# Reciprocal roots spread over the partitions by transposes of a column read with step zero, in place of a diagonal and an fp32 product

## The chip, the cores and the metric

The kernel runs on one core of a Trainium2 chip. The metric is the device time of one execution in microseconds (us); lower is better. Three runs of the kernel before gave 3015.92, 3015.95 and 3016.99 us, a median of 3015.95.

The engines of the core that matter here are PE (TensorE, the matrix engine, whose loads of the stationary operand are listed apart as PEld), DVE (VectorE), ACT (ScalarE), POOL (GpSimd) and SP (SyncE, which issues the transfers).

## The reference

One step of a two-layer hybrid encoder for 1024 prompt tokens and 64 sample tokens, in fp32. Layer 0 is a Mamba-2 state-space mixer (SSD) and a SwiGLU FFN, layer 1 a chunk-band attention and a second FFN. Every sub-layer stands between two RMS norms, and the SSD's output is normalised once more within each of four groups of channels:

```python
def rmsnorm(x, w):
    y = x * lax.rsqrt(jnp.mean(x * x, axis=-1, keepdims=True) + EPS)
    return y * w

# ssd_mixer, after the scan
yg = y.reshape(b, L, SSM_GROUPS, D_INNER // SSM_GROUPS)
yg = yg * lax.rsqrt(jnp.mean(yg * yg, axis=-1, keepdims=True) + EPS)
return (yg.reshape(b, L, D_INNER) * gnorm_w) @ w_out

# each layer
x = x + rmsnorm(mixer(rmsnorm(x, nw[0])), nw[1])
x = x + rmsnorm(swiglu(rmsnorm(x, nw[2]), ffn_w_in, ffn_w_out), nw[3])
```

The model width is 1024, the inner width of the SSD 2048.

## The kernel before

**Layout.** Features lie on the 128 partitions and tokens along the free axis, 1088 of them. Projections take them in three slices of 384, 384 and 320 tokens (`SL`), the out projections in four quarters of 256, 256, 288 and 288 (`QS`). Both operands of a matmul are split in a high and a low part, so that each tile takes three matmuls of type fp32r (lines 455 to 457, 1271 to 1273 and 1470 to 1472). The FFN uses products of sums of blocks, seven in place of eight.

**A norm's factor.** The sum of squares over features is a sum over partitions. `rstd` (L483) makes it with matmuls against a column of ones, 128 tokens at a time, into a PSUM tile `nst`. So the sums lie with tokens on partitions, one column for each 128 tokens, and nine small DVE operations (the last one L504) turn them into reciprocal roots, all but a constant factor `RL`. The column is a tile `nr`, or, for the group norms of the SSD, a place in `rst`. What follows needs the root of each token along the free axis and the same on all partitions. Before the change that takes three steps:

- `diag` (L506, its operation L508): DVE multiplies the identity with the column, block by block, which gives up to three diagonal matrices of 128x128 side by side in a tile `dg` of a ring of two (`DG`).
- `bcast` (L513, its product L516): PE multiplies a constant matrix, filled with `RL` (`frac`), with the diagonals, in fp32. All rows of the product are the roots.
- ACT copies the product from its PSUM tile `nbp` into `rb` (L520), which DVE multiplies with the data. `rb` has one buffer unless the caller gives one.

`nst` and `nbp` come out of one ring of two PSUM tiles (`ax`).

There are 44 such broadcasts: 28 from `rb_steps` (L523), which runs `rstd`, `diag` and `bcast` with pauses between for the norms in front of and behind the sub-layers (`start_norm` for the first norm, `chain` between a mixer and its FFN, `end` behind an FFN), and 16 from `build_y` (L584), for the group norms.

**Order.** PE's order is written out by hand. The main loops issue the matmuls of the projections and add their cost to a virtual clock, `st` (a `Stream`, L89). Side tasks are generators: a task yields its own cost, a delay and, where it needs one, a condition, and goes on when the virtual clock has passed the delay and the condition holds. So a delay sets how many matmuls of the main loop stand on PE between two steps of a task. The delays of `rb_steps` ahead of its broadcast are given for each caller by tables (`wait`, or else `RB_WAIT`). The other engines are ordered by priorities; `HIP` is a high one.

**`build_y`** prepares the SSD's output for its out projection: eight times (a quarter with half of the features) two blocks of four feature tiles. For a block it waits until two tiles of the ring `R` are free and the statistics of its tokens are there, broadcasts the block's roots, loads four raw tiles through SP's queue, multiplies them on DVE (L601), and writes a high part on ACT (L602) and a low part on DVE (L603), the operands of the out projection (`project`, L608). The statistics come from the SSD's tasks, which add the squares into `ssg` (L928) and call `rstd`.

**The last norm.** In `end`, for the last slice of layer 1 (`more` given), PE's matmuls `hold` (L1364) put the residual into PSUM tiles `xp` between the steps of `rb_steps`, and the scaled result is added to it there (L1373, L1375).

Of the kernel before, what the change touches and what calls it, by code (L numbers as in the profile page):

```python
# [8 lines left out]
F32 = mybir.dt.float32  # L9
F32R = mybir.dt.float32r  # L10
I32 = mybir.dt.int32
AF = mybir.ActivationFunctionType
ALU = mybir.AluOpType
# [3 lines left out]
P = 128  # L17
# [23 lines left out]
RB_WAIT = 4.8  # L41
# [9 lines left out]
HIP = 3000  # L51
# [3 lines left out]
RWP = 3000, 0, 0  # L55

KBUF = 5
DGB = 2
RAWB, HLB, SGB = 2, 3, 5
NR, NRX = 16, 13  # L60

# [6 lines left out]
RL, RP = 0.274060676, (-5.145514965, 10.804858208, -11.997578621, 8.987062454)  # L68
# [305 lines left out]
def hybrid_kernel(  # L374
# [5 lines left out]
    V, A, G, PE = nc.vector, nc.scalar, nc.gpsimd, nc.tensor  # L380
# [3 lines left out]
    def pool(es, name, bufs=1, **kw):  # L384
        return es.enter_context(tc.tile_pool(reuse_waits="tile", name=name, bufs=bufs, **kw))

    cp = pool(ctx, "cp")
# [3 lines left out]
    nsb = pool(ctx, "nsb")  # L391
# [3 lines left out]
    ident = cp.tile([P, P], F32, name="ident")  # L395
    make_identity(nc, ident)
    ones = cp.tile([P, P], F32, name="ones")
    G.memset(ones, 1.0)
    frac = cp.tile([P, P], F32, name="frac")
    G.memset(frac, RL)  # L400
    pcs = cp.tile([P, NPC], F32, name="pcs")
    A.activation(ones[:, 0:1], ones[:, 0:1], AF.Square)

# [3 lines left out]
    rst = cp.tile([P, NCH, NG], F32, name="rst")  # L407
# [9 lines left out]
    R = Ring(rp, "r", NR, [P, 1152])  # L417
# [5 lines left out]
    W.tc, W.lent = tc, Lent(RX)  # L423
    W.raws.append(W.lent)
    UC = Cells(384, (R, 99))
    DG = Ring(nsb, "dg", DGB, [P, 3, P])

    def v4(t, n):
        return t[:, :4 * n].rearrange("p (k n) -> p k n", k=4)

    def rr(ap):
        return ap.bitcast(F32R)

    def col(c):
        return pcs[:, c:c + 1]

    def ax(name):
        return pax.tile([P, 512], F32, tag="ax", name=name)

    def mm(name):  # L440
        return pmm.tile([P, 512], F32, tag="mm", name=name)
# [61 lines left out]
            V.scalar_tensor_tensor(a, a, RP[2], h, op0=ALU.add, op1=ALU.mult)  # L503
            V.scalar_tensor_tensor(r, a, RP[3], y, op0=ALU.add, op1=ALU.mult)  # L504

    def diag(r3, nb):  # L506
        dg = DG.get()
        V.tensor_tensor(  # L508
            dg[:, :nb], ident.unsqueeze(1).to_broadcast([P, nb, P]), r3.unsqueeze(2).to_broadcast([P, nb, P]), op=ALU.mult
        )  # L510
        return dg

    def bcast(dg, a, n, rb=None):  # L513

        bp = ax("nbp")
        PE.matmul(bp[:, :n], frac, dg.rearrange("p a b -> p (a b)")[:, a:a + n], start=True, stop=True)  # L516
        DG.put()
        if rb is None:
            rb = nsb.tile([P, 384], F32, tag="rb", bufs=1, name="rb")
        A.copy(rb[:, :n], bp[:, :n])  # L520
        return rb[:, :n]

    def rb_steps(ssum, n, out, wait=None, rb=None, more=None):  # L523

        nb = (n + P - 1) // P
        nr = nsb.tile([P, 4], F32, tag="nr", bufs=2, name="nr")
        rstd(ssum, 1.0 / D, nr[:, :nb], nb, more)
        yield 0.2, 0, DG.free
        with tc.high_priority(HIP):
            dg = diag(nr[:, :nb], nb)  # L530
        yield 0.1, wait or RB_WAIT
        with tc.high_priority(HIP):
            out.append(bcast(dg, 0, n, rb))
        yield 0.5, 0

    def apply_split(src, rb, wcol, n, dh, dl, eng=0):
        f = nsb.tile([P, 384], F32, tag="sq", bufs=2, name="uf")
# [12 lines left out]
    def u_slice(s):  # L550
        n = SL[s][1]
        ucells[s] = [UC.get() for _ in range(2 * KD)]
        u[s] = [(rr(ucells[s][2 * k][0][:, :n]), rr(ucells[s][2 * k + 1][0][:, :n])) for k in range(KD)]
# [26 lines left out]
    rst_done = set()  # L580
# [3 lines left out]
    def build_y():  # L584

        for q, half in ((0, 0), (1, 0), (0, 1), (1, 1), (2, 0), (3, 0), (2, 1), (3, 1)):
            o, n = QS[q]
            got = []
            c0, c1, a = ((0, 2, 0), (2, 4, 0), (4, 7, 0), (6, 9, 32))[q]
            for kh in range(2):  # L590
                g = 2 * half + kh
                yield 0, 0, lambda: R.free(2) and DG.free() and all((g, s) in rst_done for s in ((0,), (0, 1), (1, 2), (2,))[q])
                h, l_ = rr(v4(R.get(), n)), rr(v4(R.get(), n))
                dg = diag(rst[:, c0:c1, g], c1 - c0)
                yield 0, 4.0
                rb = bcast(dg, a, n)
                with tc.high_priority(BYP[q]):
                    for k in range(4):
                        t_ = stage[0]()[:, :n]
                        nc.sync.dma_start(t_, yd_[:, 4 * g + k, o:o + n])  # L600
                        V.scalar_tensor_tensor(t_, t_, col(C_GN + 4 * g + k), rb, op0=ALU.mult, op1=ALU.mult)  # L601
                        A.copy(h[:, k, :], t_)  # L602
                        V.tensor_tensor(l_[:, k, :], t_, h[:, k, :], op=ALU.subtract)  # L603
                        got.append((h[:, k, :], l_[:, k, :]))
                yield 0.5, 0
            uy[half][q] = got
# [35 lines left out]
    with ExitStack() as es:  # L642
# [400 lines left out]
        for s in range(NSL):  # L1043
            us, n = u[s], SL[s][1]
# [25 lines left out]
        for grp in order:  # L1070
# [9 lines left out]
            for i, s in seq:  # L1080
                kd_, jj_ = grp[i]
                q = 3 * jj_ + s
# [229 lines left out]
    def back(layer, start, cpost, xsrc, xmid, cpre, cpost2, xout, rb_out, done2):  # L1312
# [3 lines left out]
        with ExitStack() as es:  # L1316
# [30 lines left out]
            def end(s, y, ss, more=None):  # L1347

                o, n = SL[s]
                if s not in xss:  # L1350
                    yield from end_load(s)
                xs, xc = xss.pop(s)
                out = []
                if s == 2 and more is None:
                    yield 0, EP_W[2]
                steps = rb_steps(ss, n, out, ER_W[s], more=more)
                if more is not None:

                    xps = {}

                    def hold(ms):
                        for m in ms:
                            xps[m] = mm("xp") if m > 3 else px.tile([P, 512], F32, tag="mm", name="xp")
                            PE.matmul(xps[m][:, :n], ident, xs[m][0], start=True, stop=False)  # L1364

                    yield next(steps)
                    hold(range(4))
                    yield next(steps)
                    yield next(steps)
                    hold((4, 5))  # L1370
                    for m in range(KD):
                        ym = y[:, m, :n]
                        V.scalar_tensor_tensor(ym, ym, col(cpost2 + m), out[0], op0=ALU.mult, op1=ALU.mult)  # L1373
                        if m in xps:
                            PE.matmul(xps[m][:, :n], ident, ym, start=False, stop=True)  # L1375
                            A.copy(ym, xps[m][:, :n])
                        else:
                            V.tensor_tensor(ym, ym, xs[m][0], op=ALU.add)
                        nc.sync.dma_start(xout[:, m, o:o + n], ym)
                    for c in xs:  # L1380
                        xc.put(c)
                    yr.put()
                    return
                yield from steps
                for m in range(KD):
                    ym = y[:, m, :n]
                    with tc.high_priority(ENP[s]):
                        V.scalar_tensor_tensor(ym, ym, col(cpost2 + m), out[0], op0=ALU.mult, op1=ALU.mult)
                        V.tensor_tensor(ym, ym, xs[m][0], op=ALU.add)
                        if m % 2:  # L1390
                            nc.sync.dma_start(xout[:, m - 1:m + 1, o:o + n], y[:, m - 1:m + 1, :n])
                    yield 0, ES[s]
                for c in xs:
                    xc.put(c)
                if rb_out is None:
                    yr.put()
                    return
                yield 0, 0, lambda: UC.room(2 * KD)
                u_slice(s)

                tot = ssum_start(n)
                for m in range(KD):
                    uh, ul = u[s][m]
                    with tc.high_priority(ENP[s]):
                        A.copy(uh, y[:, m, :n])
                        V.tensor_tensor(ul, y[:, m, :n], uh, op=ALU.subtract)
                        if m % 4 == 3:
                            A.activation(y[:, m - 3:m + 1, :n], y[:, m - 3:m + 1, :n], AF.Square)
                    yield 0, ES[s]
                with tc.high_priority(ENP[s]):  # L1410
                    V.tensor_tensor(y[:, 0:4, :n], y[:, 0:4, :n], y[:, 4:8, :n], op=ALU.add)
                    V.tensor_tensor(y[:, 0:2, :n], y[:, 0:2, :n], y[:, 2:4, :n], op=ALU.add)
                    V.tensor_tensor(tot[:, :n], y[:, 0, :n], y[:, 1, :n], op=ALU.add)
                done2.append(s)
                yr.put()
                yield (0, EQ_W[s]) if s < 2 else (0, 0, lambda: "k2" in done2)
                yield from rb_steps(tot, n, [], ER_W[s], rb_out[s])
                done2.append(("rb", s))
# [35 lines left out]
            for s, (o, n) in enumerate(SL):  # L1454
# [3 lines left out]
                for m in range(KD):  # L1458
# [3 lines left out]
                    for k0, nk in KCH:  # L1462
                        w = W.get()
                        h, v = w["w"]
                        for k in range(k0, k0 + nk):
                            st.wait_for(lambda: k in hid[s])
                            xh, xl, c, cells = hid[s][k]
                            a = (k - k0) * P
# [63 lines left out]
    with ExitStack() as es:  # L1532
# [315 lines left out]
        for j in range(1, 8):  # L1848
# [6 lines left out]
            for s, i in [(s, i) for s in range(NSL) for i in range(3) if j > 1 or s == 2 or i == 2]:  # L1855
                q = 3 * j + s
# [136 lines left out]
```

## Time and profile before

| quantity | value |
|---|---|
| median of three runs | 3015.95 us (3015.92 to 3016.99) |
| span of the profiled execution | 3019.2 us |
| records in the span | 56662 |

The profiled execution is one of its own, 3.25 us longer than the median. In its rows a group of instructions is given by line, engine, operation and tile, `out<-in`, with minimum, median and maximum duration in ns. A timeline row has the start in us, the duration, the instruction, how many records it joins, and in brackets how long the engine sat idle before it and what ended that. A waits row reads: the waiting engine, tile and line; what it waited for; total us, times, longest. A row of the windows view has the stretch and its length, then busy us and count for PE, PEld, DVE, ACT and POOL, then the granted share of PE's clock, the share of the DMA engines and GB/s. The rows themselves stand in the prediction, where they are used.

### The profile page before, as it was taken

How to read it: one execution, taken by the hardware profiler on the slowest of the kernel's cores; microseconds unless marked ns; L12 is line 12 of the kernel's file. 1: busy time of each engine (PE TensorE's matmuls, PEld its weight loads, DVE VectorE, ACT ScalarE, POOL GpSimd, SP SyncE). 2: the span in 40 equal slices, each digit the busy share in tenths (PEclk: the TensorE clock that was granted, in tenths of full speed). 3: DMA queues.
4: the chain of work that ended last, by engine and by line, in shares of the span. 5: the costliest groups of instructions: out<-in, count | busy, mean ns of one | idle time of the engine just before them, and what ended most of it. 6: DMA issues, size and time to landing. Idle time of an engine off the chain costs nothing.

```text
span 3019.2 us, 56662 instructions
## 1 busy us (share of the span) xinstructions
PE 2971.5 (98%) x21803; PEld 2907.2 (96%) x21803; DVE 2047.7 (68%) x4517; ACT 1462.0 (48%) x2643; POOL 699.4 (23%) x849
## 2 busy tenths in 40 slices
PE   8999999999999999999999999999999999999999
PEld 7999999998999999999999899999999999999998
DVE  7778877785768545575546878777768655475544
ACT  6756566564443322244444666555653322244443
POOL 1333333330121334351101000000131343452111
PEclk9999999999999999999999999999999999999999
DMA  3111111124555222245655322222356222245654
GB/s 120 34 58 52 59 48 51 60 67 139 182 143 157 74 80 75 80 151 179 200 168 164 96 81 79 70 64 84 118 173 180 74 77 81 79 146 176 212 177 135
DMA packets 180671, 335.43 MB, mean 111 GB/s; under 512 B 18192, under 2 KB 128400, under 8 KB 180400
## 3 DMA queue, kind: packets, MB, share of 16 engines
q1 hardware_dynamic: 178608, 325.45, 34.5%
q0 software_dynamic: 1792, 6.36, 1.1%
q8 instruction: 171, 2.80, 0.4%
q14 instruction: 100, 0.82, 0.1%
HBM read 264.69 MB, written 62.60 MB: 108 GB/s over the span
## 4 chain that ended last, share of the span: by engine, by line
PE 85%; DVE 8%; ACT 2%; DMA 2%; issue 2%; POOL 0%; SPq 0%; DVEq 0%; ACTq 0%; POOLq 0%
PE px L1271 9%; PE px L1272 9%; PE px L1273 9%; PE mm L455 7%; PE mm L457 7%; PE mm L456 7%; PE po L1470 6%; PE po L1471 6%; PE po L1472 6%; PE mmx L455 3%; PE mmx L456 3%; PE mmx L457 3%; PE po L1754 2%; PE ptp L1715 1%; PE yp L896 1%
## 5 line engine op out<-in xcount | busy, mean ns | idle before, releaser
L455 PE MATMUL mm<-r,hl 128*128 128x384 f32 (+2 forms) x1664 | 554.9, 333 | 8.6 <-DVE dt L705 4.1
L457 PE MATMUL mm<-r,hl 128*128 128x384 f32 (+2 forms) x1664 | 540.4, 325 | 1.6 <-DVE hl L352 0.9
L456 PE MATMUL mm<-r,hl 128*128 128x384 f32 (+2 forms) x1664 | 539.4, 324 | 0.0
L340 DVE TENSOR_TENSOR hl<-raw,hl 128x1024 fp32r<-128x1024 f32 (+1 forms) x219 | 263.0, 1201 | 222.1 <-ACT hl L339 219.3
L1272 PE MATMUL px<-r,hl 128*128 128x288 f32 (+1 forms) x1184 | 348.1, 294 | 0.0
L455 PEld LDWEIGHTS mm<-r,hl 128*128 128x128 f32 x1664 | 315.8, 190 | 11.8 <-ACT BT L782 4.3
L457 PEld LDWEIGHTS mm<-r,hl 128*128 128x128 f32 x1664 | 314.9, 189 | 3.3 <-DVE hl L352 2.3
L456 PEld LDWEIGHTS mm<-r,hl 128*128 128x128 f32 x1664 | 315.7, 190 | 0.5 <-issue 0.2
L1271 PE MATMUL px<-r,hl 128*128 128x288 f32 x1056 | 311.3, 295 | 0.0
L1273 PE MATMUL px<-r,hl 128*128 128x288 f32 x1056 | 311.3, 295 | 0.0
L339 ACT CAST hl<-raw 128x1024 fp32r<-128x1024 f32 (+1 forms) x219 | 219.1, 1005 | 179.5 <-PE po L1472 102.9
L481 POOL TENSOR_TENSOR ssum<-ssum,sq 128x256 f32<-128x256 f32 (+3 forms) x97 | 128.0, 1320 | 656.3 <-ACT sq L480 643.1
L1272 PEld LDWEIGHTS px<-r,hl 128*128 128x128 f32 x1184 | 222.7, 188 | 0.0
L1273 PE MATMUL px<-rx,hl 128*128 128x256 f32 x768 | 215.9, 281 | 5.1 <-DVE hl L340 5.1
L1271 PE MATMUL px<-rx,hl 128*128 128x256 f32 x768 | 216.5, 282 | 0.7 <-ACT hl L339 0.7
L1471 PE MATMUL po<-rx,hl 128*128 128x384 f32 (+1 forms) x624 | 202.0, 324 | 0.4 <-DVE rx L1335 0.3
L1470 PE MATMUL po<-rx,hl 128*128 128x384 f32 (+1 forms) x608 | 198.6, 327 | 0.6 <-ACT rx L1334 0.6
L1271 PEld LDWEIGHTS px<-r,hl 128*128 128x128 f32 x1056 | 198.6, 188 | 0.4 <-DVE u L1286 0.3
L1273 PEld LDWEIGHTS px<-r,hl 128*128 128x128 f32 x1056 | 198.6, 188 | 0.0
L1472 PE MATMUL po<-rx,hl 128*128 128x384 f32 (+1 forms) x608 | 196.9, 324 | 0.0
L1272 PE MATMUL px<-rx,hl 128*128 128x256 f32 x640 | 179.6, 281 | 0.0
L289 POOL TENSOR_TENSOR tt<-raw 128x512 f32<-128x512 f32 x40 | 54.8, 1369 | 449.5 <-DMA raw<-in_w_f_dram 311.6
(364 smaller groups left out, 8197.6 us busy)
## 6 DMA issues: line engine op xcount, KB each, us to landing
raw<-in_w_f_dram SPq DMA_DIRECT2D x154, 512.0 KB, 3.7
rx<-in_w_f_dram SPq DMA_DIRECT2D x54, 512.0 KB, 3.7
raw<-in_w_in_dram SPq DMA_DIRECT2D x40, 512.0 KB, 3.6
sg<-hscr SPq DMA_DIRECT2D x88, 192.0 KB, 3.6
raw<-in_w_f_dram SPq DMA_DIRECT2D x44, 384.0 KB, 3.3
raw<-in_w_so_dram SPq DMA_DIRECT2D x32, 512.0 KB, 3.8
raw<-in_w_kv_dram SPq DMA_DIRECT2D x18, 512.0 KB, 3.6
raw<-in_w_o_dram SPq DMA_DIRECT2D x16, 512.0 KB, 3.7
```

What stands on the lines that cost most here:

```text
L339: self.nc.scalar.copy(h, v)
L340: (eng or self.eng or self.nc.vector).tensor_tensor(lo, v, h, op=ALU.subtract)
L455: PE.matmul(ps[:, :n], h_, xh, start=(first and i == 0), stop=False)
L456: PE.matmul(ps[:, :n], h_, xl, start=False, stop=False)
L457: PE.matmul(ps[:, :n], l_, xh, start=False, stop=(last and i == nk - 1))
L481: (eng or G).tensor_tensor(ssum[:, :n], ssum[:, :n], q[:, :n], op=ALU.add)
L1271: PE.matmul(ps, wh, ah[:, k, :], start=(k == 0), stop=False)
L1272: PE.matmul(ps, wh, al[:, k, :], start=False, stop=False)
L1273: PE.matmul(ps, wl, ah[:, k, :], start=False, stop=(k == 3))
L1470: PE.matmul(ps[:, :n], wh, xh, start=(k == 0), stop=False)
L1471: PE.matmul(ps[:, :n], wh, xl, start=False, stop=False)
L1472: PE.matmul(ps[:, :n], wl, xh, start=False, stop=(k == FT - 1))
```

## The change

The diagonals, their ring and the constant matrix go. `bcast` now takes the column itself: for each 128 tokens PE transposes a 128x128 operand that reads one column with step zero along its free axis, so that all its columns are the same and all rows of the transpose are the roots. ACT's copy becomes an activation that scales by `RL`. A chunk of tokens is always a full 128, so a broadcast is two transposes (the quarters of 256) or three (all others); the activation reads only the tokens that are wanted, from column `a` on.

The pauses of the tasks change with it. `rb_steps` had three (0.2 with a wait for the ring, 0.1 with the caller's delay, 0.5) and has two (0.3 with the caller's delay, 0.35). `build_y` paused for 4.0 between the diagonal and the broadcast and now pauses for 2.5 ahead of the broadcast, without the ring's condition. `end` keeps its matmuls of the residual at the place where they were, between the statistics and the broadcast.

```diff
-DGB = 2
...
-    frac = cp.tile([P, P], F32, name="frac")
-    G.memset(frac, RL)
...
-    DG = Ring(nsb, "dg", DGB, [P, 3, P])
...
-    def diag(r3, nb):
-        dg = DG.get()
-        V.tensor_tensor(
-            dg[:, :nb], ident.unsqueeze(1).to_broadcast([P, nb, P]), r3.unsqueeze(2).to_broadcast([P, nb, P]), op=ALU.mult
-        )
-        return dg
-
-    def bcast(dg, a, n, rb=None):
+    def bcast(r, a, n, rb=None):
 
         bp = ax("nbp")
-        PE.matmul(bp[:, :n], frac, dg.rearrange("p a b -> p (a b)")[:, a:a + n], start=True, stop=True)
-        DG.put()
+        for i in range((a + n + P - 1) // P):
+            PE.transpose(bp[:, i * P:(i + 1) * P], r[:, i:i + 1].to_broadcast([P, P]), ident)
         if rb is None:
             rb = nsb.tile([P, 384], F32, tag="rb", bufs=1, name="rb")
-        A.copy(rb[:, :n], bp[:, :n])
+        A.activation(rb[:, :n], bp[:, a:a + n], AF.Copy, scale=RL)
         return rb[:, :n]
 
     def rb_steps(ssum, n, out, wait=None, rb=None, more=None):
...
-        yield 0.2, 0, DG.free
+        yield 0.3, wait or RB_WAIT
         with tc.high_priority(HIP):
-            dg = diag(nr[:, :nb], nb)
-        yield 0.1, wait or RB_WAIT
-        with tc.high_priority(HIP):
-            out.append(bcast(dg, 0, n, rb))
-        yield 0.5, 0
+            out.append(bcast(nr, 0, n, rb))
+        yield 0.35, 0
...
-                yield 0, 0, lambda: R.free(2) and DG.free() and all((g, s) in rst_done for s in ((0,), (0, 1), (1, 2), (2,))[q])
+                yield 0, 0, lambda: R.free(2) and all((g, s) in rst_done for s in ((0,), (0, 1), (1, 2), (2,))[q])
                 h, l_ = rr(v4(R.get(), n)), rr(v4(R.get(), n))
-                dg = diag(rst[:, c0:c1, g], c1 - c0)
-                yield 0, 4.0
-                rb = bcast(dg, a, n)
+                yield 0, 2.5
+                rb = bcast(rst[:, c0:c1, g], a, n)
...
-                    yield next(steps)
+                    got = next(steps)
                     hold(range(4))
-                    yield next(steps)
+                    yield got
                     yield next(steps)
```

## The prediction

> **What bounds the kernel now.** First the page: span, busy time and the chain that ended last, then the clock by core.
>
> ```profile
> span 3019.2 us, 56662 instructions
> PE 2971.5 (98%) x21803; PEld 2907.2 (96%) x21803; DVE 2047.7 (68%) x4517; ACT 1462.0 (48%) x2643; POOL 699.4 (23%) x849
> PE 85%; DVE 8%; ACT 2%; DMA 2%; issue 2%; POOL 0%; SPq 0%; DVEq 0%; ACTq 0%; POOLq 0%
> core 0: 3019.2 us, clock 0.995
> ```
>
> PE is busy for 98% and carries 85% of the chain, at nearly full clock. So PE time saved comes off the end wherever PE is the limit, while DVE (68%) and ACT (48%) count only where PE waits. The profiled span is 3.25 us above the median of the runs (3015.95 us). The sum below is made within the span, and its difference is taken off the median.
>
> The waits of PE show where it isn't the limit. Two of them lie in the stretch that ends the SSD (660 to 700 us), and both wait for DVE's statistics:
>
> ```profile
> PE nst L489 <- DVE ssg L928: 2.9, 2, 1.6
> PE mm L455 <- DVE nv L503: 1.4, 1, 1.4
> ```
>
> Then the groups of the tiles that the change touches, and of three tiles that stand in for the new operation:
>
> ```profile
> L516 PEld LDWEIGHTS nbp<-dg,frac x88: 185/188/337, 30.6 to 3009.4; 128*128 128x128 f32 x88
> L516 PE MATMUL nbp<-dg,frac x88: 377/405/799, 30.7 to 3009.7; 128*128 128x256 f32 x32, 128*128 128x288 f32 x32, 128*128 128x384 f32 x16, 128*128 128x320 f32 x8
> L520 ACT COPY rb<-nbp x41: 364/398/492, 31.6 to 3010.2; 128x256 f32<-128x256 f32 x16, 128x288 f32<-128x288 f32 x16, 128x384 f32<-128x384 f32 x6, 128x320 f32<-128x320 f32 x3
> L508 DVE TENSOR_TENSOR dg<-ident,nr x28: 412/557/561, 26.2 to 3008.7; 128x384 f32<-128x384 f32 x20, 128x256 f32<-128x256 f32 x8
> L508 DVE TENSOR_TENSOR dg<-ident,rst x16: 414/546/1132, 232.0 to 844.8; 128x256 f32<-128x256 f32 x8, 128x384 f32<-128x384 f32 x8
> L830 PEld LDWEIGHTS xtp<-ident,xsT x144: 138/141/146, 90.1 to 657.6; 128*128 128x128 f32 x144
> L830 PE MATMUL xtp<-ident,xsT x144: 271/273/328, 90.1 to 657.7; 128*128 128x128 f32 x144
> L847 PEld LDWEIGHTS bcp<-acr,sel x96: 185/191/193, 90.4 to 659.0; 128*128 128x128 f32 x96
> ```
>
> The 88 records of L516 are 44 broadcasts: an fp32 product leaves two, one for each pass. By width they are 16 of 256, 16 of 288, 8 of 384 and 4 of 320. An fp32 transpose leaves one record: L830's 48 tasks make three each.
>
> **The change, part by part.**
>
> *PE.* Each broadcast is now two transposes (the 256s) or three (the others): 16x2 + 28x3 = 116. Records overlap, so a cost is read from starts: from the broadcast's to the one at which the old pace is back, less what the ordinary matmuls between take.
>
> ```profile
> 30.57 0.33 PE L741 MATMUL dtp<-r,dtw 128*64 128x384 f32 x1
> 30.74 0.81 PE L516 MATMUL nbp<-dg,frac 128*128 128x384 f32 x2
> 31.09 0.63 PE L740 MATMUL dtp<-r,dtw 128*64 128x384 f32 x1
> 31.55 0.34 PE L741 MATMUL dtp<-r,dtw 128*64 128x384 f32 x1
> ...
> 736.38 0.28 PE L457 MATMUL mmx<-r,hl 128*128 128x256 f32 x1
> 736.50 0.59 PE L516 MATMUL nbp<-dg,frac 128*128 128x256 f32 x2
> 736.74 0.47 PE L455 MATMUL mmx<-r,hl 128*128 128x256 f32 x1
> 737.05 0.28 PE L456 MATMUL mmx<-r,hl 128*128 128x256 f32 x1
> ...
> 758.94 0.65 PE L516 MATMUL nbp<-dg,frac 128*128 128x288 f32 x2
> 759.21 0.49 PE L455 MATMUL mmx<-r,hx 128*128 128x256 f32 x1
> 759.55 0.28 PE L456 MATMUL mmx<-r,hx 128*128 128x256 f32 x1
> ```
>
> A 384-wide matmul takes 0.17 (30.57 to 30.74), a 256-wide one 0.12 (736.38 to 736.50). So the 384 broadcast costs 31.55 - 30.74 - 0.17 = 0.64 us, the 256 one 737.05 - 736.50 - 0.12 = 0.43, the 288 one 759.55 - 758.94 - 0.12 = 0.49; 320 lies between them, at about 0.53. Together 16x0.43 + 16x0.49 + 8x0.64 + 4x0.53 = 22.0 us.
>
> Three fp32 transposes in the same kind of stream:
>
> ```profile
> 51.31 0.49 PE L799 MATMUL bnp<-ident,BT 128*128 128x128 f32 x3
> 51.56 0.42 PE L455 MATMUL mm<-r,hl 128*128 128x384 f32 x1
> 51.82 0.33 PE L456 MATMUL mm<-r,hl 128*128 128x384 f32 x1
> ```
>
> They cost 51.82 - 51.31 - 0.17 = 0.34 us, 0.113 each. 116 of them are 13.1 us, so PE's own work falls by 8.9 us. I take 7.1: 0.8 belongs to two broadcasts of 384 and one of 320 that are counted with their stalls below, and about 1.0 lies in the SSD's last stretch, where PE waits for DVE anyway. Bounds 6.5 and 8.1.
>
> No transpose of before reads a column with step zero. The nearest rows are L830's (full tile, load 141 ns) and L847's, whose fp32r operand is read with step zero and loads in 191 ns, as the 188 of L516 does without. I take 0.113 us, by L799; the far ends are the rivals.
>
> The Trainium skill ("TensorE: Matmul & The Clock Gate", "🔬 Part 4: PE-mode transpose") gives about 275 ns for one such transpose within a kernel and says that its time doesn't count as busy for full clock. The 273 ns of L830 agree as a record's length; the starts at 51.31 to 51.82 show that three don't take three such lengths. By 275 ns each the transposes would be an estimated 31.9 us and the PE term a loss of 9.9.
>
> *DVE.* 28x0.557 + 16x0.546 = 24.3 us of diagonals go, and with them the ring of two. DVE has 32% to spare, so they count only where PE waits behind one: twice, below, and at the end.
>
> *ACT.* The 44 copies (398 ns) become activations with a scale that read the same columns. I take no difference: ACT is idle 52%, and its copy is read by DVE work that is ahead of PE except at the end. At most the span between 364 and 398 there, 0.03 us either way, in the last term's bounds.
>
> *The first norm.* PE waits for the second column and the diagonals between:
>
> ```profile
> 45.63 0.56 DVE L508 TENSOR_TENSOR dg<-ident,nr 128x384 f32<-128x384 f32 x1
> 46.10 0.15 DVE L504 SCALAR_TENSOR_TENSOR nr<-nv 128x3 f32<-128x3 f32 x1
> 46.33 2.26 PE L516 MATMUL nbp<-dg,frac 128*128 128x384 f32 x4 [2.31 <-DVE nr L504]
> 46.30:50.00 3.70, 3.67 (x10) 2.87 (x11) 2.10 (x5) 1.72 (x4) 0.56 (x3) 0.56 0.02 4
> ```
>
> Without the first diagonal the second column ends some 0.5 earlier, and the transposes may start at about 45.8. The windows row shows PE at 0.56 of its clock after this stall; it stays, since a wait of 1.8 us is left. The two products run 46.33 to 47.93, six transposes at half clock 1.36. Gain 0.5 + 0.24 = 0.7; up to 1.4 if the shorter stall leaves full clock. I take 1.0.
>
> *The scheduler's order.* `build_y` makes the 16 gated-norm blocks of the out projection. It now asks for 2.5 us of PE work ahead of its broadcast where 4.0 stood, and has no diagonal before it, so its broadcasts move ahead in PE's hand-written order: in the first eight the fourth stands at matmul 3862 in place of 3892, the eighth at 3919 in place of 3979. All the rest stays within 14 matmuls. What was late:
>
> ```profile
> 742.68 0.59 PE L516 MATMUL nbp<-dg,frac 128*128 128x256 f32 x2
> 746.62 0.39 PE L456 MATMUL mmx<-r,hl 128*128 128x256 f32 x1 [0.24 <-DVE r L603]
> 748.34 0.39 PE L455 MATMUL mmx<-r,hl 128*128 128x256 f32 x1 [0.86 <-ACT r L602]
> 749.10 0.38 PE L456 MATMUL mmx<-r,hl 128*128 128x256 f32 x1 [0.38 <-DVE r L603]
> 749.80:753.40 3.60, 3.60 (x18) 3.31 (x17) 1.65 (x2) 1.36 (x2) 0.00 (x0) 0.53 0.36 90
> ```
>
> The eighth broadcast is issued 4 us ahead of the first matmul that waits for its block. The stalls are 1.48 us, and the clock of 0.53 in the next 3.6 us costs more. From 745.86, where the old pace ends, to 753.38, where it returns, lie 7.52 us; the 26 matmuls and one broadcast in it would take 26x0.12 + 0.49 = 3.6. So 3.9 are lost. 60 matmuls earlier are 7.2 us, more than the lateness. But the block's raw rows stand behind the same two weight loads in SP's queue in both programs, so part may stay late: 0 to 3.9, and I take 3.0. The low clock after a stall is the one seen at 46 us.
>
> The Trainium skill (same page, "No PE-idle gaps >~3µs between matmul bursts", in "🎯 Why this matters for your kernels") would have no half clock after waits this short; the 0.53 here, after 1.48 us in three pieces, differs. By it the place would be worth an estimated 1.5 and the sum 10.8.
>
> The same move puts four blocks' worth of DVE work (four products and four roundings more, two diagonals fewer, some 1.9 us) ahead of the statistics for which PE waits at the SSD's end (the 2.9 and 1.4 us above). DVE itself waits there for about 2.5, so it may vanish into that: 0, between -1.9 and +1.9.
>
> *Two more places.* One broadcast late in layer 1 waits for its diagonal, and the last one of all:
>
> ```profile
> 2245.75 0.70 PE L516 MATMUL nbp<-dg,frac 128*128 128x256 f32 x2 [0.95 <-DVE dg L508]
> ...
> 3008.70 0.56 DVE L508 TENSOR_TENSOR dg<-ident,nr 128x384 f32<-128x384 f32 x1
> 3009.32 0.81 PE L516 MATMUL nbp<-dg,frac 128*128 128x320 f32 x2 [0.16 <-DVE dg L508]
> ```
>
> The first saves 0.5 of its 0.95 at least (a diagonal's length), 0.95 at most: 0.7. In the tail the column is ready at 3008.70, but PE works until 3009.16: 0.16 goes, and three transposes (2x0.113 + 0.273 = 0.50) end where 0.81 stood. 0.47, so 0.5 (0.4 to 0.6).
>
> **Sum.** 7.1 + 1.0 + 3.0 + 0 + 0.7 + 0.5 = 12.3 us less: span 3006.9, time 3015.95 - 12.3 = 3003.6. All upper bounds: 8.1 + 1.4 + 3.9 + 1.9 + 0.95 + 0.6 = 16.9, 2999.1.
>
> **The rivals.**
>
> 1. *The new order gives back what it takes.* The earlier blocks delay the SSD's last statistics by the full 1.9 us, and the block at 748 stays late behind its load. For: that stretch waits for DVE by the two rows above, and the DMA share is 0.36 just there. Against: the eighth block has 7.2 us. 7.1 + 1.0 - 1.9 + 0 + 0.7 + 0.5 = 7.4: 3008.6.
>
> 2. *The step-zero load sets the pace.* If a column read with step zero loads in L847's 191 ns and is not overlapped, 116x(0.191 - 0.113) = 9.0 us go: 12.3 - 9.0 = 3.3, 3012.6. Against: L847's 191 and L516's 188 are loads of another mode, and the ordinary ones hide behind streams of 0.12.
>
> 3. *Transposes in a row don't overlap.* 116x0.273 = 31.7 in place of 22.0, a loss of 9.7, while the other places gain 5.2: 4.5 more, 3020.5. It is what the Trainium skill's 275 ns would mean. Against: L799's starts.
>
> 4. *Slower: neither load nor stream overlaps,* if each transpose of such a column waits with its load until the stream before it has ended. 116x(0.141 + 0.273) = 48.0, a loss of 26.0 less 5.2: 20.8 more, 3036.8. It decides from 27.2/116 = 0.235 us for one transpose (22.0 + 5.2 to be spent). For: no row has an fp32 transpose of such a column. Against: L847 reads that way without a penalty.
>
> That the change leaves the work as it is can be ruled out: diagonals and products leave the program.
>
> **How the numbers follow.** Forecast 0.66, rival 1 0.19, rival 2 0.06, rival 3 0.02, rival 4 0.07. A measurement here can't tell 0.2%, 6.0 us, from none. Faster by more (below 3009.9): the forecast and three quarters of rival 1, 0.80. Within: the rest of rival 1, rivals 2 and 3, 0.13. Slower: 0.07. The range goes from the upper bounds (2999) over rival 1 to 3011, leaving out rivals 2 to 4 (0.15) and a little at the ends. The forecast's own range is 2999 to 3008.
>
> **What would show it.** Starts around a 256 broadcast: 0.23 us in place of 0.43, around a 384 one 0.34 in place of 0.64. PE's first transpose after 43.7 at about 45.8. No half clock at 746 to 753; the statistics' waits near 690 no longer than now. No wait at 2245. Wrong would be: a transpose's load above 141 ns, transposes 0.19 or more apart, a new wait of PE for ACT's copy of `nbp`, or new stalls where the blocks' order moved.

## The result, and the profile after

The changed kernel took 3007.2 us in the median of six runs (3003.36 to 3009.09), against 3015.99 (3015.87 to 3016.99): 8.8 us less, a ratio of 0.9969 with a 95% interval of 0.9958 to 0.9980. It was timed twice more beside the experiments, on two chips: 3004.93 against 3018.28 (0.9957, 0.9944 to 0.9971) and 3007.39 against 3017.54 (0.9964, 0.9952 to 0.9977). The three ratios are 9 to 13 us; the forecast was 12.3, its rival 1 had 7.4. The first measurement is nearer to the rival, the other two (13.0 and 10.9 us) are nearer to the forecast.

First the profile page after (span, busy time, chain by engine) and the groups of `nbp`:

```profile
span 3005.0 us, 56685 instructions
PE 2958.7 (98%) x21831; PEld 2903.3 (97%) x21831; DVE 2026.7 (67%) x4473; ACT 1461.0 (49%) x2643; POOL 699.3 (23%) x848
PE 90%; DVE 5%; DMA 2%; ACT 2%; issue 1%; POOL 0%; SPq 0%; DVEq 0%; POOLq 0%; ACTq 0%
...
L506 PEld LDWEIGHTS nbp<-ident,nr x76: 133/135/138, 29.3 to 2995.5; 128*128 128x128 f32 x76
L506 PE MATMUL nbp<-ident,nr x76: 269/272/294, 29.5 to 2995.7; 128*128 128x128 f32 x76
L509 ACT ACTIVATE rb<-nbp x41: 362/404/493, 30.0 to 2996.0; 128x256 f32<-128x256 f32 x16, 128x288 f32<-128x288 f32 x16, 128x384 f32<-128x384 f32 x6, 128x320 f32<-128x320 f32 x3
L506 PE MATMUL nbp<-ident,rst x40: 270/272/455, 656.8 to 837.4; 128*128 128x128 f32 x40
```

PE is as full as before, with 116 transposes (76 + 40) of one record each in place of 88 records of the product. A step-zero column loads in 135 ns, less than the 141 of the full tile before, and streams in the same 272. DVE's busy time is 21 us less. ACT's activations take 404 ns where the copies took 398.

The profiled span went from 3019.2 to 3005.0 us, 14.2 less, more than the medians did. The difference by stage, from the start of the same PE instruction in the two timelines, shows where it arose. The kernel before was profiled a second time, as was the changed one twice; the experiments stand beside them and are told below. Each column ends at an instruction whose start in the first profile of before is given; negative is faster; the last one is the tail. Each mark is an instruction that has the same number of other PE records ahead of it, broadcasts aside, in all kernels of the table: a mark that itself moved in PE's order would count the move as time.

| us, against the first profile of before | 40 | 54 | 665 | 690 | 802 | 938 | 1648 | 1735 | 2219 | 2260 | 3005 | tail |
|---|---|---|---|---|---|---|---|---|---|---|---|---|
| before, second profile | -0.3 | 0.0 | -0.1 | 0.1 | 0.2 | 0.0 | -0.3 | -0.8 | 0.8 | 0.0 | -0.2 | 0.0 |
| after | -1.6 | -2.8 | 1.7 | 2.4 | -5.8 | -2.3 | -4.0 | 4.1 | -2.3 | -1.8 | -1.1 | -0.6 |
| after, second | -1.6 | -2.8 | -0.6 | 2.4 | -5.9 | -2.3 | -4.2 | 4.3 | -1.1 | -1.8 | -1.2 | -0.7 |
| after, third | -1.6 | -2.8 | -0.8 | 2.4 | -3.3 | -2.3 | -3.7 | 4.9 | -2.8 | -1.8 | -1.0 | -0.7 |
| e1: transposes, pauses of before | -0.1 | -2.8 | 3.5 | 0.4 | -3.8 | -0.2 | -4.1 | 0.5 | -2.4 | -1.0 | -0.2 | -0.7 |
| e2: products, pause 2.5 | -1.6 | 0.0 | -0.6 | 4.3 | -4.2 | 0.1 | -2.5 | -0.6 | 0.8 | 0.0 | 0.2 | 0.0 |
| e3: after, pause 4.0 | -1.8 | -2.8 | 1.9 | 0.2 | -3.8 | -1.2 | -4.4 | 3.3 | -2.3 | -1.8 | -0.7 | -0.6 |
| e9: after, attention's order kept | -1.8 | -2.8 | -0.4 | 2.4 | -5.7 | -2.3 | -2.3 | -0.3 | -1.2 | -2.1 | -0.5 | -0.7 |

Two stages are slower in every profile of the changed kernel, the end of the SSD (665 to 690) and the start of the attention (1648 to 1735); nearly all the rest gains. Not all of a gain is the change's. Up to 40 us e2 has the same instructions as before, yet is 1.6 us ahead. The same stretch in the windows view, of before's second profile and then of e2 (PE's clock stands ahead of the last two figures):

```profile
22.50:26.00 3.50, 3.50 (x13) 3.50 (x12) 3.50 (x16) 3.21 (x9) 0.00 (x0) 0.51 0.93 298
```

```profile
22.50:26.00 3.50, 3.50 (x22) 3.50 (x21) 3.50 (x15) 3.40 (x9) 0.00 (x0) 1.00 0.87 303
```

The clock is 0.51 there and 1.00 here, with nothing changed ahead of it. (The last section says what differs.)

### The profile page after: what moved, and what is told of

It is laid out like the page before. It is cut to its first block, busy times and chain, and to the rows that moved or that the text cites. A ratio compares the mean times of both kernels' runs of the same rounds, so it can differ in the third digit from the quotient of the medians.

```text
span 3005.0 us, 56685 instructions
## 1 busy us (share of the span) xinstructions
PE 2958.7 (98%) x21831; PEld 2903.3 (97%) x21831; DVE 2026.7 (67%) x4473; ACT 1461.0 (49%) x2643; POOL 699.3 (23%) x848
## 4 chain that ended last, share of the span: by engine, by line
PE 90%; DVE 5%; DMA 2%; ACT 2%; issue 1%; POOL 0%; SPq 0%; DVEq 0%; POOLq 0%; ACTq 0%
PE px L1256 9%; PE px L1257 9%; PE px L1258 9%; PE mm L451 8%; PE mm L453 8%; PE mm L452 8%; PE po L1456 6%; PE po L1455 6%; PE po L1457 6%; PE mmx L451 4%; PE mmx L452 4%; PE mmx L453 4%; PE po L1739 2%; PE ptp L1700 2%; PE yp L881 1%
```

## The experiments

All fractions are against the kernel before, run beside them on the same chip. Four groups follow, then what they say of the forecast.

**Is it the order, or the transposes?** e1 puts all pauses back, e3 only that of `build_y`, e2 makes only that edit in the kernel before.

```diff
 # e1, in the changed kernel
-        yield 0.3, wait or RB_WAIT
+        yield 0.2, 0
+        yield 0.1, wait or RB_WAIT
...
-        yield 0.35, 0
+        yield 0.5, 0
...
-                yield 0, 2.5
+                yield 0, 4.0
...
-                    got = next(steps)
+                    yield next(steps)
                     hold(range(4))
-                    yield got
+                    yield next(steps)
                     yield next(steps)
 # e2, in the kernel before
-                yield 0, 4.0
+                yield 0, 2.5
 # e3, in the changed kernel
-                yield 0, 2.5
+                yield 0, 4.0
```

> Transposes, but all pauses of the tasks as before, so that PE's order is that of before. Theory of the forecast (the order was worth 3.0 us): 3007.2 + 3.0 = 3010.2 us. Rival (the new order gives back what it takes, a loss of 1.9): 3005.3 us, with PE's waits for the SSD's last statistics near 680 us as short as before (1.3 to 1.6 us each) and the late block's stalls at 746 to 749 still there.

> The kernel before with one number changed: 2.5 for 4.0 in build_y; diagonals and products stay. Theory of the forecast (the order is worth 3.0 us): 3016.0 - 3.0 = 3013.0 us, no half clock at 749 us. Rival (the order costs 1.9): 3017.9 us, a longer wait for ssg near 680 us.

> The changed kernel with one number put back: 4.0 for 2.5 in build_y. If build_y's pause is all of the order's effect, the time is that of the run with all pauses of before: 3010.2 us by the forecast, 3005.3 by the rival. If the pauses of rb_steps matter, it differs from that run by more than 2 us.

Measured: e1 3007.84 us (0.9961, 0.9949 to 0.9974), e3 3007.64 (0.9961, 0.9948 to 0.9973), e2 3017.88 against 3018.43 (0.9997, 0.9988 to 1.0005). So the transposes with the old order bring about all of it, and the new pause alone nothing that can be told from zero. Neither number of the forecast or its rival is hit for e1. The second timing of the changed kernel, 3004.93 us, lies 2.9 us below e1, but on another chip; by the ratios, 0.9957 and 0.9961, it is 1 us, within the intervals. The table shows why the pause is worth so little: the pause of 2.5 loses at one place what it gains at the next. PE's waits between 655 and 702 us, of the changed kernel first, then of e3:

```profile
PE nst L485 <- DVE ssg L913: 3.2, 1, 3.2
PE nst L485 <- DVE nv L492: 0.8, 1, 0.8
PE mm L451 <- DVE zs L720: 0.8, 1, 0.8
```

```profile
PE nst L485 <- DVE ssg L913: 2.8, 2, 1.7
PE mm L451 <- DVE zs L720: 2.6, 2, 1.6
```

The totals are much the same (4.8 and 5.4 us), but with 2.5 there is one long wait of 3.2 us, and PE has 0.59 of its clock in the stretch after it, as the windows view of the changed kernel shows (the last figures are clock, DMA share and GB/s):

```profile
685.00:690.60 5.60, 5.60 (x31) 5.53 (x31) 5.07 (x21) 2.36 (x7) 0.00 (x0) 0.59 0.38 112
```

From 665 to 690 the changed kernel loses 2.4 us and e3 0.2; from 690 to 802 it gains 5.8 and e3 3.8, since e3's low clock comes later (0.70 from 687.6 to 693.2). Up to 802 the two come out even; from 802 to 938 the changed kernel gains 2.3 and e3 1.2. In all, from 665 to 938, the pause brings 1.0 us in two profiles and loses 1.5 in the third.

The forecast took 3.0 for the late block, most of it for the low clock behind its stalls. That low clock went without the new order as well. From 735 to 754 us, measured as in the table, the changed kernel gains 2.8 us (2.8 and 0.3 in the other two profiles), but e1 and e3, with the old pause, gain 2.3 each, and e2, with the new pause and the products, 2.2. (Where they are transposes, the three broadcasts' own saving is an estimated 0.5 of it.) In e3's windows view the place is at full clock:

```profile
740.00:752.00 12.00, 10.84 (x84) 10.05 (x84) 10.45 (x22) 7.04 (x16) 2.39 (x3) 1.00 0.62 196
```

And the late block stayed late. PE's waits from 735 to 760 us, in e2 and in the changed kernel:

```profile
PE mmx L456 <- DVE r L603: 1.0, 2, 0.7
```

```profile
PE mmx L451 <- ACT r L587: 0.6, 1, 0.6
PE mmx L452 <- DVE r L588: 0.4, 1, 0.4
```

e2, whose broadcast is as early as in the changed kernel, still has 1.0 of the 1.48 us there, the changed kernel 1.1 (1.1 and 1.9 in the other two profiles); e1 and e3, whose broadcast is as late as before, have 0.9 and 1.1. What holds the block in the changed kernel is its load, as the row of DVE's timeline says; the last broadcast of 256 is long done there:

```profile
740.71 0.88 DVE L586 SCALAR_TENSOR_TENSOR sg<-sg,pcs,rb 128x256 f32<-128x256 f32 x2 [1.14 <-DMA sg<-yscr]
```

DVE stood idle for 1.14 us until the raw rows landed. Before's half clock at 749 came back in its second profile; the changed kernel has none there in two profiles and has it in the third, from 744.5 on, in the windows view:

```profile
744.50:748.50 4.00, 4.00 (x21) 4.00 (x22) 3.71 (x8) 2.37 (x5) 0.00 (x0) 0.57 0.64 208
```

That third profile gained only 3.3 us in the stage to 802 where the others have 5.8 and 5.9. So the earlier order didn't rid the kernel of this risk, and the stall is no shorter with it than without. Why it is shorter in e1 and e3 than in before stays open.

**What a transpose costs.** e4 issues each transpose twice, e7 adds one of a full tile of ones ahead of each.

```diff
 # e4
+            for _ in range(2):
                 PE.transpose(bp[:, i * P:(i + 1) * P], r[:, i:i + 1].to_broadcast([P, P]), ident)
 # e7
+            PE.transpose(bp[:, i * P:(i + 1) * P], ones, ident)
             PE.transpose(bp[:, i * P:(i + 1) * P], r[:, i:i + 1].to_broadcast([P, P]), ident)
```

> Each of the 116 transposes is issued twice into the same place, so PE does 116 more. By the forecast's 0.113 us each: 13.1 more, 3020.3 us. If a load of the step-zero column sets the pace (0.191): 22.2 more, 3029.4. If neither load nor stream overlaps (0.414): 48.0 more, 3055.

> 116 more transposes, as in the run with each issued twice, but the added ones read a full tile of ones instead of the column with step zero. If a step-zero column costs nothing extra: the same as that run, 3018.9 us. If it does (0.191 against 0.113 us): some 9 us less than that run, 3010.

Measured: e4 3018.91 us (0.9999, 0.9990 to 1.0008), e7 3018.68 (1.0003, 0.9994 to 1.0012). Against the mean of the three ratios of the changed kernel, 0.9963, that is 0.0036 and 0.0040 of 3018 us: 11 and 12 us for 116 more transposes, near 0.1 us each. The difference between the two is within their intervals, so a step-zero column costs nothing extra that these runs can show. The timeline of e7 shows it without any comparison; ones and column alternate:

```profile
30.25 0.27 PE L506 MATMUL nbp<-ident,ones 128*128 128x128 f32 x1
30.36 0.27 PE L507 MATMUL nbp<-ident,nr 128*128 128x128 f32 x1
30.47 0.27 PE L506 MATMUL nbp<-ident,ones 128*128 128x128 f32 x1
30.58 0.27 PE L507 MATMUL nbp<-ident,nr 128*128 128x128 f32 x1
```

Each starts 0.11 us after the one before, though each record is 0.27 long: a record's length is no price where records overlap.

**What the diagonals cost DVE.** e6 and e11 are one kernel, run twice: the changed one, with the diagonals made again and not read.

```diff
+    def dummy(r3, nb):
+        dg = nsb.tile([P, 3, P], F32, tag="dg", bufs=2, name="dg")
+        V.tensor_tensor(
+            dg[:, :nb], ident.unsqueeze(1).to_broadcast([P, nb, P]), r3.unsqueeze(2).to_broadcast([P, nb, P]), op=ALU.mult
+        )
...
         rstd(ssum, 1.0 / D, nr[:, :nb], nb, more)
+        with tc.high_priority(HIP):
+            dummy(nr[:, :nb], nb)
...
+                dummy(rst[:, c0:c1, g], c1 - c0)
                 yield 0, 2.5
```

> The changed kernel with DVE's 44 diagonals put back at their old places, but read by nobody. By the forecast DVE's load counts only where something on PE's path stands behind a diagonal: 0.5 us at the first norm (the second column behind the first diagonal), 3008 us in all. Rival (DVE's 24 us count wherever DVE is full, in the SSD up to 660 us and at its end): 3 us or more, 3010.5 us and above.

> The unread diagonals once more: their first median lay 3.8 us above that of the changed kernel, while the two profiled spans were equal (3003.9 and 3003.8). If DVE's load itself costs: again 3 us or more above the changed kernel beside it. If the difference was spread: within 1.5 us of it.

Measured: 3008.74 us (0.9973, 0.9964 to 0.9982) and 3006.48 (0.9964, 0.9951 to 0.9976), beside 3004.93 and 3007.39 of the changed kernel. The first difference (3.8 us) didn't repeat; the second is -0.9, and the profiled spans are 3003.9 and 3004.7 against 3003.8 and 3005.7. At the first norm the two profiles gain 2.5 and 2.4 us where the changed kernel has 2.8, near the 0.5 that was expected there. In all, DVE's diagonals by themselves cost nothing that these runs can show.

**The two stages that became slower.** e8 delays the last group's statistics, e9 splits one pause of `rb_steps` as before, which restores the order of PE's work at the start of the attention.

```diff
 # e8, in the changed kernel
-                yield 0, 5.0
+                yield 0, 8.0 if j == XT - 1 else 5.0
 # e9, in the changed kernel
-        yield 0.3, wait or RB_WAIT
+        yield 0.2, 0
+        yield 0.1, wait or RB_WAIT
...
-                    got = next(steps)
+                    yield next(steps)
                     hold(range(4))
-                    yield got
+                    yield next(steps)
                     yield next(steps)
```

> The changed kernel with 8.0 in place of 5.0 as the pause ahead of the last group's statistics, so that 24 more matmuls stand on PE ahead of one of them. If PE's waits of 3.2 and 0.8 us for ssg near 680 us are the price of the order of the last SSD tasks: 2 to 3 us less, 3005. Rival (the blocks behind those statistics become as much later): no change, 3007.6 us.

> The changed kernel with one pause of rb_steps split as before (0.2, then 0.1 with the caller's delay), which puts the order of PE's work at the start of the attention back to that of before; the pause of build_y stays at 2.5. Theory: the reordered start of the attention (new waits for hl of 2.2 and for mx of 1.9 us near 1700 us, and low clock behind them) costs 2 to 3.5 us, so 2 to 3.5 us less than the changed kernel beside it, with S and pT waits near 1710 us as before. Rival (those waits fall on another place, or are within the spread): no difference above 1 us.

> The changed kernel once more, as the base on the same chip for the runs beside it: 3005 to 3007 us if the chips agree.

e8: 3007.66 us (0.9967, 0.9956 to 0.9979), no gain. The wait for `ssg` went, and this stands in its place in the waits of the same stretch. It is for ACT's copy of a finished tile of the out projection (L608), which stood behind roundings on ACT that had waited 2.27 us for DVE:

```profile
PE mm L451 <- ACT r L608: 4.2, 1, 4.2
PE nst L485 <- DVE nv L489: 1.2, 1, 1.2
```

e9: 3003.21 us (3002.07 to 3006.09), ratio 0.9953 (0.9939 to 0.9966), the fastest of all; the changed kernel beside it had 3007.39 (e10). That is 4.2 us less, though the two intervals overlap. PE's waits between 1690 and 1740 us in before, and at the same place in the changed kernel and in e9:

```profile
PE S L1683 <- DVE pT L1720: 1.8, 3, 0.9
PE mm L455 <- DVE kf L1585: 1.3, 1, 1.3
PE mm L457 <- DVE hl L352: 0.5, 2, 0.3
```

```profile
PE ptp L1700 <- DVE mx L1678: 2.2, 2, 1.9
PE mm L453 <- DVE hl L351: 2.2, 1, 2.2
PE mm L451 <- DVE kf L1570: 1.2, 1, 1.2
```

```profile
PE S L1669 <- DVE pT L1706: 1.8, 3, 0.9
PE mm L451 <- DVE kf L1571: 1.5, 1, 1.5
PE mm L453 <- DVE hl L351: 0.5, 2, 0.3
```

The new order put scores (`S`) ahead of projections there: short waits for `pT` and `hl` gave way to two of about 2 us, with low clock behind them, while the wait for `kf` is there in all three. In the table the stage costs the changed kernel 4.1 to 4.9 us and e3, with the same order, 3.3; the profiles of e4, e6, e7, e8 and e11, which have it too, lie between 2.8 and 4.9. In e1, e2 and e9, which have before's order, it costs 0.5 or less. So the reordering costs 3 to 5 us there.

The medians of e1 and e3 don't show it (3007.84 and 3007.64), though e1 has before's order here and e3 the new one. By the table e1 loses elsewhere what it saves: 1.0 us from 802 to 938, 0.8 from 2219 to 2260 and 0.5 up to 3005. e1 also has the old last pause of `rb_steps` (0.5 for 0.35), which e9 has not.

The last profile is of the kernel before.

> The kernel before, profiled once more. If the half clock after 46 and after 749 us belongs to these stalls it is there again (0.5 to 0.6 of the clock in both stretches); if it depends on the moment it is gone in one of them, and the forecast's two terms for them (1.0 and 3.0 us) held only for that one execution.

Its span was 3018.7 us. The windows view shows both stretches of half clock again:

```profile
46.00:49.70 3.70, 3.62 (x9) 2.79 (x10) 2.04 (x5) 1.63 (x4) 0.56 (x3) 0.56 0.01 4
749.30:752.90 3.60, 3.60 (x19) 3.46 (x19) 1.65 (x2) 1.36 (x2) 0.00 (x0) 0.54 0.29 84
```

## Why the prediction was right, step by step

**PE's own work (7.1 of 8.9): right.** The timeline of the changed kernel around a 384 broadcast and a 256 one:

```profile
29.45 0.49 PE L506 MATMUL nbp<-ident,nr 128*128 128x128 f32 x3
29.70 0.42 PE L725 MATMUL dtp<-r,dtw 128*64 128x384 f32 x1
29.95 0.34 PE L726 MATMUL dtp<-r,dtw 128*64 128x384 f32 x1
...
734.11 0.38 PE L506 MATMUL nbp<-ident,rst 128*128 128x128 f32 x2
734.24 0.36 PE L451 MATMUL mmx<-r,hl 128*128 128x256 f32 x1
734.45 0.28 PE L452 MATMUL mmx<-r,hl 128*128 128x256 f32 x1
```

29.95 - 29.45 - 0.17 = 0.33 us where 0.64 stood, 734.45 - 734.11 - 0.12 = 0.22 where 0.43 stood: the forecast's 0.34 and 0.23. e4 and e7 rule out rivals 2, 3 and 4 (0.191, 0.273 and 0.414 us each). The 275 ns of the Trainium skill ("TensorE: Matmul & The Clock Gate", "🔬 Part 4: PE-mode transpose"), which are given there for bf16, agree with the record's 272 of an fp32 one, but the time that a transpose adds is 0.11 us.

**The first norm (1.0): right in kind, too small.** It brought 2.8 us in all three profiles. The first transposes after the wait, in the changed kernel, and the products at the same place in before's second profile:

```profile
44.14 0.84 PE L506 MATMUL nbp<-ident,nr 128*128 128x128 f32 x6 [1.72 <-DVE nv L499]
44.73 0.42 PE L451 MATMUL mm<-r,hl 128*128 128x384 f32 x1
44.99 0.34 PE L452 MATMUL mm<-r,hl 128*128 128x384 f32 x1
```

```profile
46.08 2.30 PE L516 MATMUL nbp<-dg,frac 128*128 128x384 f32 x4 [2.31 <-DVE nr L504]
```

The wait fell by 0.6 us as forecast (a diagonal's length), but the term took half clock behind it for granted. At 1.72 us of wait PE went on at full clock (the second matmul is 0.26 us behind the first, as in the rows at 51.56 and 51.82 before), and that was the larger part of the gain. The forecast had full clock as its upper bound and put that at 1.4; the matmuls behind the products, which also ran at half clock until 50 us, weren't in it.

**The order (3.0, and 0 for DVE's work ahead of the statistics): wrong.** The two together brought 1.0 us in two profiles and -1.5 in the third (the changed kernel against e3, 665 to 938), which the runs' times can't tell from zero. Two steps failed. The late block's low clock went in e1 and e3 too, which have the old order, so its going isn't the order's doing. And the earlier blocks did delay the statistics: the waits near 690, which were to be no longer than before, became one of 3.2 us, and PE lost 2.4 us up to there. That price stood in the forecast as a bound of 1.9 and as rival 1; it should have been taken with the gain, since one move causes both. That the block's load holds it back was named as the reason for less than 3.9, and the wait of 1.14 us for it is there. The reading of the order was off as well: by the traces the broadcast at 742.68 moved ahead by 48 matmuls (5.8 us at 0.12), and it is the one at 700.08 that moved by 60; the two behind the late block, at 752 and 759, moved by 72 and 96, not by up to 14.

**The start of the attention (not in the sum): missed.** "All the rest stays within 14 matmuls" was said of the broadcasts; the tasks of the attention moved too, and cost 3 to 5 us. No term of the forecast stands for it. Nothing in the timing of before shows it: it needs the listing of the order on PE, read for all tiles and not for `nbp` alone.

**Layer 1's late broadcast (0.7): right in size, for another reason.** The wait of 0.95 is gone. (The stage up to 2260 brought 1.8 us, but the broadcasts' own saving is in it, about 0.2 each.) In e1, which has no diagonal but the old order, the wait is still there, in its waits:

```profile
PE nbp L506 <- DVE nr L500: 0.9, 1, 0.9
```

So the new places removed it, and not the diagonal's going: in the changed kernel the statistics stand 12 matmuls later and the broadcast 16 records later. e3 puts the pause of `build_y` back and e9 splits the one ahead of the broadcast as before; both have these new places and no wait, so it is the shorter last pause of `rb_steps` that moved them. e1 gains 1.0 in that stage.

**The tail (0.5): right.** 0.6 to 0.7 in all runs with the transposes once.

That the sum came out near is thus partly luck: 1.8 too little at the first norm and 0.3 at the late broadcast, against 2 to 5 too much for the order and 3 to 5 missed. The remainder is in low clock that falls in one execution and not in another: at the late block, which lost it without the order, and in the stages up to 40, 665 and 1648. This also spreads the runs of the changed kernel over 5.7 us.

## What to carry to other kernels

A broadcast of a column over the partitions by a transpose of the column read with step zero costs PE about half of an fp32 product with a diagonal, and makes another engine's work on the diagonal needless; price it by the distance between starts, not by the records' length. Where pauses of tasks change with an edit, list the whole order of PE's work before and after: a difference in a task far from the edit (here the attention's start, 3 to 5 us) can take back a good part of the gain. A delay that is shortened at one place may only move the same wait, so try it alone in the old kernel, as e2 does. And where stages of two profiles are compared, take as marks instructions that didn't move in the order.

## What the runs showed of the hardware

A wait decides over more than its own length. At the first norm, after 2.31 us without work PE ran at about half clock in all three profiles with products (0.56 of its clock in the two of before), and after 1.72 us at full clock in every profile with transposes that had that wait, ten in all.

Where a wait falls counts too. In the clock records of the 14 profiles the clock is half or full, and it changes only at steps of 3.413 us: within an execution all stretches at half clock start a whole number of such steps apart, to within 0.02 us, and last one, two or three of them (the last one ends with the span). Where the steps lie differs from execution to execution. All 14 profiles have two waits, of 1.26 and 0.51 us, near 121 us. In five of them both waits lie within one step, and the next step is at half clock in all five; in eight a border lies between the two, and all eight stay at full clock; in one a border divides the second wait, and half clock follows. The step behind these waits in the first profile of the changed kernel, and the same place in its second:

```profile
122.95:126.35 3.40, 3.40 (x12) 3.40 (x11) 3.40 (x11) 2.26 (x3) 0.00 (x0) 0.50 0.00 0
```

```profile
120.80:124.15 3.35, 2.85 (x16) 2.85 (x17) 3.04 (x9) 2.86 (x4) 0.00 (x0) 1.00 0.00 0
```

At 22 us, in before's two profiles the wait of 1.6 us lies within one step and half clock follows; in e2 a border divides it. One step at half clock costs up to half its length, 1.7 us, and which places are hit changes from run to run.

No bound on the idle time of a step fits all places. The 1.77 us near 121 brought half clock. The 1.72 of the first norm, whole within one step in eight profiles, didn't, nor did the 1.6 at 22 us in three profiles where it ends with its step (the second and third of the changed kernel, and e9). But the 1.4 and 1.5 us that lie in one step near 749 in before's two profiles did. The rule of the Trainium skill that the forecast weighed ("TensorE: Matmul & The Clock Gate", "🎯 Why this matters for your kernels", only gaps of some 3 us bring half clock) doesn't hold at 2.31 us, in three profiles of three.
